# First weights between the pieces of the memory, squares and conv sums on GpSimd, five u blocks loaded ahead of their stage

## The chip, the cores and the metric

The kernel runs on one core of a Trainium2 chip, in one launch. A core has five engines that each work through a list of instructions in order: TensorE (PE, matmuls, with its weight loads as PEld), VectorE (DVE), ScalarE (ACT), GpSimd (POOL) and SyncE (SP), and 16 DMA engines that the transfers of all queues share. The metric is the device time of one execution in microseconds.

## The reference

256 tokens of 1024 numbers pass two blocks. All arithmetic is float32.

```
h = rms_norm(x, norm_g);  mem_h = rms_norm(mem, mem_norm_g)      # 256 x 1024 each
c_glu, c_gate, d_q, d_k, d_v, d_gate, x_q, x_gate, merge = split(h @ w_in)
y_conv = silu(layer_norm(conv31(a * sigmoid(b)) + dw_b)) * silu(c_gate) @ w_conv_proj
y_diff = differential attention(d_q, d_k, d_v), normed, * silu(d_gate) @ w_diff_proj
y_mem  = attention(x_q; k, v = split(mem_h @ w_mem_kv)) * silu(x_gate) @ w_x_proj
x = x + (g0 * y_conv + g1 * y_diff + g2 * y_mem) @ w_out         # g = sigmoid(merge)

h = rms_norm(x, norm_mix);  q, k, v, x_rg, g_rg = split(h @ w_in_2)
x = x + concat(norm(stick breaking attention), norm(rg_lru(conv4(x_rg)) * gelu(g_rg))) @ w_out_2
h = rms_norm(x, norm_ffn)
s = (h @ w_query) . sub_keys                                     # 8 heads, 2 x 128 keys
idx, gate = the 16 best of (top 16 of half 1) + (top 16 of half 2), softmax
x = x + sum_k gate_k * gelu(h . u[idx_k]) * v[idx_k]             # 16384 experts
```

rms_norm divides by the root of the mean square over the 1024 channels; layer_norm needs the mean and the mean square over the channels of the conv's output.

## The kernel before, in words

Channels lie on the 128 partitions, in eight chunks; a tile of one chunk is 128 x 256 (channels x tokens). Every dense product is cut into weight blocks of 1024 x 256, stored as 128 x 2048 and loaded in two halves of 512 KB. There are 94 such blocks of ordinary weights (in_wcat, 188 halves) and then 64 blocks of u and 64 of v, all experts of the last layer.

An ordinary block goes through `prep`: SyncE loads a half (raw), ScalarE rounds it to the short format (whi, L247), VectorE subtracts (wlo = raw - whi, L248), and TensorE multiplies three times: whi with the high part of the activations (hh), wlo with hh, whi with the low part (hl). One block is 48 matmuls into a PSUM tile called lin, of which there are three. `linT` gives channels x tokens, `linN` (L330) tokens x channels. `ahead` starts the preparation of the block behind the one just multiplied.

The start. SyncE loads the memory m_t in four pieces (256 KB each) with the vectors VT behind the first, then the first weights, then x in two halves, tables, and more weights. ScalarE scales m_t by its gain into mgh and rounds it, VectorE forms the rest mgl; ScalarE squares the four pieces, and eight matmuls with a matrix of ones (L439) add up the squares over the channels (tile stat). Then come blocks 0 to 3 (mem_h times the value half of w_mem_kv). Meanwhile x gets its norm, and hh and hl are made from it; blocks 4 and 5 are the first to use them.

The conv. Each of the 31 taps of the first layer's conv is one VectorE instruction per chunk (L533, L535, 248 in all) that accumulates into cacc. The taps lie in a list bg from which some are issued behind each block, so they fill VectorE's time between the wlo subtractions. When all are done, ScalarE squares cacc and TensorE adds cacc and its squares up over the channels (L691 to L699: eight matmuls on cacc, eight on the squares, float32), then VectorE forms mean and variance, ScalarE the reciprocal root (rv, rs, rt). Between them stand the blocks mc1 to mc3 (gates, the sigmoids smc), and behind these four blocks cg0 to cg3.

Each activation function of ScalarE belongs to a table, and a change of table is an instruction of its own (ACT_TABLE_LOAD). A list scheduler sets the order of all instructions on each engine by priorities and estimated ready times, so an edit at one place can change orders at others.

The expert layer. Of the 256 tokens 160 are worked densely: TensorE multiplies them with all 64 blocks of u (L288) and, weighted by the gates, all 64 of v (L1177), in float32, without rounding; these halves are loaded into a ring of 13 tiles, the former raw, whi and wlo tiles (`prep_plain`, L225). The gates come from products A and B (group gp), and VectorE multiplies them in (`mul`, L1155). The other 96 tokens are gathered: GpSimd issues 96 indirect loads of u rows and 96 of v rows (L1186, 512 KB each), VectorE forms a dot product of each u tile (L1193) and accumulates each v tile (L1211). VectorE's list mixes these with the ga operations of L1155, and a gather's buffer comes free only when VectorE has used it. The tile ga is the place for the results of the u blocks.

GpSimd does nothing before 597 us; then it loads fold, copies xG, adds the candidate sums cs of the top-k (L998), and issues the gathers.

## Time and profile before

| | |
|---|---|
| runs | 1292.05, 1288.19, 1291.8 us, median 1291.8 |
| profiled execution | 1291.35 us, span 1289.6 us |
| TensorE busy | 1253.5 us (97% of the span) |
| VectorE busy | 937.0 us (73%) |
| ScalarE busy | 457.3 us (35%) |
| GpSimd busy | 214.6 us (17%) |
| DMA | 340.76 MB, mean 264 GB/s |

A row of the timeline gives the start of an instruction in us from the start of the span, its length, engine, line and operation, output <- inputs by name, the shapes, and in brackets how long the engine was idle before it and what ended that. Where several alike follow each other they stand in one row with their count. Matmul records overlap, so the length of one says less than the distance between them. A digit in the slices is the busy share in tenths of 1289.6 / 40 = 32.2 us. A DMA share of 1 means that all 16 DMA engines are busy.

### The profile page before, as it was taken

What the parts mean: (1) busy time and instruction counts of PE and PEld (TensorE: products, weight loads), DVE (VectorE), ACT (ScalarE), POOL (GpSimd) and SP (SyncE); (2) the same over time, 40 slices, a digit from 0 to 9 for tenths busy, and PEclk for the clock granted to TensorE, in tenths of its full rate; (3) what the DMA queues carried; (4) which work ended last, traced back from release to release, by engine and by line L of the source; (5) the groups of instructions that cost most, each with busy time, mean ns of one, the idle gap of its engine ahead of it and who ended that gap; (6) DMA issues with size and microseconds to landing.
All of it is one profiled execution on the core that took longest, in us unless ns stands there. A gap on an engine that the chain in (4) does not pass through costs nothing.

```text
span 1289.6 us, 24478 instructions
## 1 busy us (share of the span) xinstructions
PE 1253.5 (97%) x9948; PEld 1211.0 (94%) x9948; DVE 937.0 (73%) x1806; ACT 457.3 (35%) x741; POOL 214.6 (17%) x222
## 2 busy tenths in 40 slices
PE   8999999999999999998999899999999999999995
PEld 7999999989999999977999899999999999999884
DVE  6889988888998777855899864588545886445444
ACT  7545677578646556955431100010000000000001
POOL 0000000000000000000013443222342225333331
PEclk9999999999999999999999999999999999999998
DMA  8655443434565664423577999999999999999996
GB/s 294 189 194 182 164 138 124 132 116 147 164 200 161 196 202 157 148 67 99 181 235 240 354 409 409 409 408 363 382 383 342 356 360 392 409 409 408 409 409 231
DMA packets 94865, 340.76 MB, mean 264 GB/s; under 512 B 10576, under 2 KB 12048, under 8 KB 94624
## 3 DMA queue, kind: packets, MB, share of 16 engines
q1 hardware_dynamic: 66752, 237.98, 52.0%
q0 software_dynamic: 28000, 101.22, 20.4%
q8 instruction: 78, 1.28, 0.4%
q14 instruction: 35, 0.29, 0.1%
HBM read 338.01 MB, written 1.05 MB: 263 GB/s over the span
## 4 chain that ended last, share of the span: by engine, by line
PE 43%; issue 20%; DMA 16%; DVE 11%; POOL 6%; ACT 3%; POOLq 0%; SPq 0%; DVEq 0%; ACTq 0%
DMA gat<-in_vrow,gi 10%; PE lin L308 10%; PE lin L307 10%; PE lin L309 10%; POOL gat L1186 6%; DMA gat<-in_urow,gi 5%; DVE acc L1211 2%; PE lin L341 1%; DVE gat L1193 1%; PE lin L343 1%; PE lin L342 1%; DVE wlo L248 1%; PE stat L459 1%; ACT whi L247 1%; DVE I L983 1%
## 5 line engine op out<-in xcount | busy, mean ns | idle before, releaser
L1177 PE MATMUL y<-ga,w 128*128 128x160 f32 x2048 | 293.0, 302 | 5.6 <-DMA w<-in_v 2.8
L1177 PEld LDWEIGHTS y<-ga,w 128*128 128x128 f32 x2048 | 279.9, 190 | 13.3 <-DMA w<-in_v 10.4
L288 PE MATMUL lin<-h3f,w 128*128 128x160 f32 x2048 | 290.5, 302 | 1.7 <-ACT ga L1166 1.7
L288 PEld LDWEIGHTS lin<-h3f,w 128*128 128x128 f32 x2048 | 281.5, 191 | 2.3 <-ACT ga L1166 1.9
L248 DVE TENSOR_TENSOR wlo<-raw,whi 128x1024 fp32r<-128x1024 f32 x188 | 229.1, 1221 | 64.2 <-ACT whi L247 63.5
L247 ACT CAST whi<-raw 128x1024 fp32r<-128x1024 f32 x188 | 196.2, 1049 | 167.2 <-PE lin L308 123.8
L308 PE MATMUL lin<-hl,whi 128*128 128x256 f32 x704 | 200.2, 284 | 0.0
L309 PE MATMUL lin<-hh,wlo 128*128 128x256 f32 x704 | 199.8, 284 | 0.0
L307 PE MATMUL lin<-hh,whi 128*128 128x256 f32 x704 | 199.8, 284 | 0.0
L1211 DVE SCALAR_TENSOR_TENSOR acc<-gat,cG,acc 128x1024 f32<-128x1024 f32 x94 | 120.7, 1284 | 95.3 <-DMA gat<-in_vrow,gi 49.2
L1193 DVE CUSTOM_DVE_ANT_0 gat<-gat,hrow 128x1024 f32<-128x1024 f32 x96 | 116.6, 1224 | 29.8 <-DMA gat<-in_urow,gi 16.2
L1186 POOL DMA_INDIRECT gat<-in_urow,gi x96 | 103.4, 1077 | 198.9 <-DVE sG L1193 188.9
L309 PEld LDWEIGHTS lin<-hh,wlo 128*128 128x128 f32 x704 | 132.6, 188 | 2.2 <-issue 1.9
L308 PEld LDWEIGHTS lin<-hl,whi 128*128 128x128 f32 x704 | 132.6, 188 | 1.7 <-issue 1.4
L307 PEld LDWEIGHTS lin<-hh,whi 128*128 128x128 f32 x704 | 132.5, 188 | 1.4 <-issue 1.0
L1186 POOL DMA_INDIRECT gat<-in_vrow,gi x96 | 93.3, 972 | 162.6 <-DVE acc L1211 127.4
L1166 ACT ACTIVATE ga<-lin 128x320 f32<-128x320 f32 x64 | 27.9, 437 | 249.8 <-PE lin L288 216.7
L535 DVE SCALAR_TENSOR_TENSOR cacc<-ub,VT,cacc 128x256 f32<-128x256 f32 x240 | 103.7, 478 | 0.0
L955 POOL DMA_DIRECT2D fold<-in_con x1 | 0.7, 703 | 596.9 <-DVE gate L924 596.9
L1292 ACT COPY ga<-y 128x160 f32<-128x160 f32 x4 | 1.2, 292 | 236.2 <-PE y L1177 236.2
L1155 DVE SCALAR_TENSOR_TENSOR ga<-gp,ga 128x256 f32<-128x256 f32 (+1 forms) x60 | 29.1, 510 | 74.6 <-PE gp L1144 55.3
L308 PE MATMUL lin<-h3lo,whi 128*128 128x256 f32 x128 | 37.3, 291 | 2.3 <-DVE h3lo L384 2.3
(373 smaller groups left out, 2099.9 us busy)
## 6 DMA issues: line engine op xcount, KB each, us to landing
raw<-in_wcat SPq DMA_DIRECT2D x188, 512.0 KB
w<-in_u SPq DMA_DIRECT2D x128, 512.0 KB
w<-in_v SPq DMA_DIRECT2D x128, 512.0 KB
gat<-in_urow,gi POOLq DMA_INDIRECT x96
gat<-in_vrow,gi POOLq DMA_INDIRECT x96
m_t<-in_memT SPq DMA_DIRECT2D x4, 256.0 KB
xr<-in_xT SPq DMA_DIRECT2D x2, 512.0 KB
kT<-in_keysT SPq DMA_DIRECT2D x1, 1024.0 KB
```

What stands on the lines that cost most here:

```text
L247: nc.scalar.copy(h, raw)
L248: state["sub"] = nc.vector.tensor_sub(l, raw, h.bitcast(F32))
L288: nc.tensor.matmul(ps[:, a], ws[a][:, c * P:(c + 1) * P], x[:, c], start=c == 0, stop=c == 7)
L307: nc.tensor.matmul(ps[:, a], wh, ah[:, c], start=(a, c) in first, stop=False)
L308: nc.tensor.matmul(ps[:, a], wh, al[:, c], start=False, stop=False)
L309: nc.tensor.matmul(ps[:, a], wl, ah[:, c], start=False, stop=(a, c) in last)
L535: nc.vector.scalar_tensor_tensor(cacc[:, c], s, w, cacc[:, c], op0=ALU.mult, op1=ALU.add)
L1155: state["dve"] = nc.vector.scalar_tensor_tensor(g_[:, :, tl], p_, 1.0 / GSCALE, g_[:, :, tl], op0=ALU.mult, op1=ALU.mult)
L1177: nc.tensor.matmul(yT[c // 2][:, c % 2, :D], ws[a][:, c * P:(c + 1) * P], g[:, a], start=False, stop=i == 63 and (a, c % 2) == (1, 1))
L1186: nc.gpsimd.indirect_dma_start(g, None, src, bass.IndirectOffsetOnAxis(gi[:, 0, k:k + 1].bitcast(U32), 0))
L1193: nc.vector.tensor_tensor_reduce(out=g, in0=g, in1=h, scale=1.0, scalar=0.0, op0=ALU.mult, op1=ALU.add, accum_out=sG[:, k:k + 1])
L1211: state["sum"] = nc.vector.scalar_tensor_tensor(acc[m], g, cG[:, k:k + 1], acc[m], op0=ALU.mult, op1=ALU.add)
```

## The change

The edits are these.

- The first weights' halves are loaded between the pieces of m_t, the second block's weights ahead of x. Block 0 is multiplied channel by channel for both token halves.
- The four squares of m_t and two of the adds go to GpSimd; TensorE adds up the first piece's squares ahead of block 0 and the sum of the other three behind it. The norm of m_t is formed there.
- The sums over cacc are formed while the taps run: ScalarE squares a pair of chunks as soon as it is done, GpSimd (for the first three pairs) or VectorE (the last) adds up rx and sqs. Three matmuls remain of sixteen.
- ScalarE's operations for la (a constant of the second block) stand behind the last merge sigmoid.
- u blocks 11 to 15 (LATE) are not loaded through the ring, but by ten transfers that GpSimd issues ahead of the fold load, into parts of ga that are not yet in use.

```diff
         NW = len(STREAM)
+        LATE = range(NW + 11, NW + 16)
         RING = ("raw",) * 5 + ("whi",) * 4 + ("wlo",) * 4
 
         def prep_plain(i):
             ws = []
             for a in range(2):
-                tag = RING[(2 * (i - NW) + a) % len(RING)]
+                tag = RING[(2 * (i - NW - (len(LATE) if i >= LATE.stop else 0)) + a) % len(RING)]
                 w = spool.tile([P, 1024], F32, name="w", tag=tag, bufs=RING.count(tag))
                 nc.sync.dma_start(w, srcs[i][:, a * 1024:(a + 1) * 1024])
                 ws.append(w)
             prepared[i] = ws
 
-        def prep(i):
+        def load(i, a):
+            raw = spool.tile([P, 1024], F32, name="raw", bufs=5)
+            nc.sync.dma_start(raw, srcs[i][:, a * 1024:(a + 1) * 1024])
+            return raw
...
-            for j in range(i, min(i + (5 if i >= NW else 1), len(srcs))):
+            n = 5 + (i - 1 in LATE) if i >= NW else 1
+            for j in [j for j in range(i, len(srcs)) if j not in LATE][:n]:
...
+                nc.tensor.matmul(ps[:, t], xh, wh, start=(t, c) in first, stop=False)
+                nc.tensor.matmul(ps[:, t], xl, wh, start=False, stop=False)
+                nc.tensor.matmul(ps[:, t], xh, wl, start=False, stop=(t, c) in last)
...
+            def m_load(k):
+                nc.sync.dma_start(m_t[:, 2 * k:2 * k + 2], memT[:, 2 * k:2 * k + 2])
+
+            m_load(0)
             nc.sync.dma_start(VT, vec)
-            for k in range(1, 4):
-                nc.sync.dma_start(m_t[:, 2 * k:2 * k + 2], memT[:, 2 * k:2 * k + 2])
-            prep(0)
+            raws = [load(0, 0)]
+            m_load(1)
+            m_load(2)
+            raws.append(load(0, 1))
+            m_load(3)
+            raws1 = [load(1, a) for a in range(2)]
             for k in range(2):
                 nc.sync.dma_start(x_t[:, 4 * k:4 * k + 4], xT[:, 4 * k:4 * k + 4])
+            mgh, mgl = bigt("mgh", F32R), bigt("mgl", F32R)
+
+            def m_gains(a):
+                for c in range(4 * a, 4 * a + 2):
+                    gain_col(m_t, "mem_norm_g", mgh, mgl, c)
+
+            m_gains(0)
+            prep(0, raws, lambda a: [gain_col(m_t, "mem_norm_g", mgh, mgl, c) for c in (2, 3, 4, 5)] if a else None)
+            for c in (6, 7):
+                gain_col(m_t, "mem_norm_g", mgh, mgl, c)
+
+            stm = statp()
+            msq = [smt("sqs", 512, 1), smt("sq"), smt("sq")]
+            for k in range(4):
+                q = msq[min(k, 2)] if k < 3 else smt("gate", 512, 3)
+                nc.gpsimd.tensor_mul(q.rearrange("p (a b) -> p a b", a=2), m_t[:, 2 * k:2 * k + 2],
+                                     m_t[:, 2 * k:2 * k + 2])
+                if k > 1:
+                    nc.gpsimd.tensor_add(msq[1], msq[1], q)
+                if k == 0:
+                    for b in range(2):
+                        nc.tensor.matmul(stm[:, :T], ONES, q[:, b * T:(b + 1) * T], start=b == 0, stop=False)
+            rm = smt("rm", T, 1)
+            prep(1, raws1)
...
-            for c in range(0, NC, 2):
-                rms_sq(m_t, stm, c, NC)
-            rstd_of(stm[:, :T], 1.0 / 1024, T, out=rm)
-            rmt = tok_scalar(rm, "rmt")
             vm = big.tile([P, 2, 1024], F32, name="vm", tag="big")
             hh, hl = bigt("hh", F32R), bigt("hl", F32R)
             for j in range(4):
-                ps = linN((mgh, mgl))
+                ps = linN((mgh, mgl), j == 0)
+                if j == 0:
+                    for b in range(2):
+                        nc.tensor.matmul(stm[:, :T], ONES, msq[1][:, b * T:(b + 1) * T], start=False, stop=b == 1)
+                    rstd_of(stm[:, :T], 1.0 / 1024, T, out=rm)
+                    rmt = tok_scalar(rm, "rmt")
...
+            def conv_sums(j):
+
+                def f():
+                    e = nc.gpsimd if j < 3 else nc.vector
+                    x = cacc[:, 2 * j:2 * j + 2]
+                    sq = smt("sq" if j else "sqs", 512, 2 if j else 1)
+                    nc.scalar.square(sq.rearrange("p (a b) -> p a b", a=2), x)
+                    if j == 0:
+                        sums.append(sq)
+                        e.tensor_add(rx, x[:, 0], x[:, 1])
+                    else:
+                        for k in range(2):
+                            e.tensor_add(rx, rx, x[:, k])
+                        e.tensor_add(sums[0], sums[0], sq)
+                return f
+
             for j in range(4):
                 pb = linT(h)
                 sg = smt("sig")
@@ -546,6 +604,7 @@
                 for jj in range(KT):
                     for c in (2 * j, 2 * j + 1):
                         bg.append((0.394, tap(c, jj)))
+                bg.append((0.0, conv_sums(j)))
...
-            for c in range(0, NC, 2):
-                sq = smt("sq")
-                nc.scalar.square(sq.rearrange("p (a b) -> p a b", a=2), cacc[:, c:c + 2])
-                for k in range(2):
-                    nc.tensor.matmul(s1[:, :T], ONES, cacc[:, c + k], start=c + k == 0, stop=c + k == 7)
-                    nc.tensor.matmul(s2[:, :T], ONES, sq[:, k * T:(k + 1) * T], start=c + k == 0, stop=c + k == 7)
+            nc.tensor.matmul(s1[:, :T], ONES, rx, start=True, stop=True)
+            for k in range(2):
+                nc.tensor.matmul(s2[:, :T], ONES, sums[0][:, k * T:(k + 1) * T], start=k == 0, stop=k == 1)
...
+        late = [g[:, o:o + 32].rearrange("p a b -> p (a b)") for g, o in ((ga[0], 32), (ga[1], 0))]
+        late = [x[:, k * 1024:(k + 1) * 1024] for x in late for k in range(len(LATE))]
+        for k, i in enumerate(LATE):
+            for a in range(2):
+                nc.gpsimd.dma_start(late[2 * k + a], srcs[i][:, a * 1024:(a + 1) * 1024])
+            prepared[i] = late[2 * k:2 * k + 2]
```

The order of GpSimd's instructions before, up to its first add (m_t is the memory, cs the top-k's candidate sums):

```order
L1305 MEMSET const-uint8-127 128x1
L1313 UNCONDITIONAL_BRANCH
L955 DMA fold<-in_con 128x96
L956 COPY xG<-xr 128x768
L998 ISA
L998 TENSOR_TENSOR cs<-V_7191 128x256 x11
```

And now:

```order
L522 ISA
L522 TENSOR_TENSOR sqs<-m_t 128x512
L522 TENSOR_TENSOR sq<-m_t 128x512 x2
L525 TENSOR_TENSOR sq<-sq 128x512
L522 TENSOR_TENSOR gate<-m_t 128x512
L525 TENSOR_TENSOR sq<-sq,gate 128x512
L589 TENSOR_TENSOR rx<-cacc 128x256
L592 TENSOR_TENSOR rx<-rx,cacc 128x256 x2
L593 TENSOR_TENSOR sqs<-sqs,sq 128x512
L592 TENSOR_TENSOR rx<-rx,cacc 128x256 x2
L593 TENSOR_TENSOR sqs<-sqs,sq 128x512
L1005 DMA ga_7127<-in_u 128x1024 x5
```

GpSimd now has six instructions on m_t at the start, seven on the conv's sums, and ten loads of u, all ahead of fold.

ScalarE in the stretch of the differential attention between the norm of one head pair (rv, rs, rt) and the copy of its neighbour's probabilities (sig<-att), before:

```order
L374 ACTIVATE rv<-stat,VT 128x512
L662 ACTIVATE gate<-lin 128x512
L375 ACT_TABLE_LOAD
L375 ACTIVATE rs<-rv 128x512
L376 ACT_TABLE_LOAD
L376 ACTIVATE rs<-rs 128x512
L570 ACTIVATE pp,z<-s,nm 128x128 x2
L377 ACTIVATE rt<-rs 128x512
L643 COPY sig<-att 128x384
L570 ACTIVATE pp,z<-s,nm 128x256 x2
L247 CAST whi<-raw 128x1024 x4
```

And now:

```order
L387 ACTIVATE rv<-stat,VT 128x512
L388 ACT_TABLE_LOAD
L388 ACTIVATE rs<-rv 128x512
L254 CAST whi<-raw 128x1024
L721 ACT_TABLE_LOAD
L721 ACTIVATE gate<-lin 128x512
L629 ACT_TABLE_LOAD
L629 ACTIVATE pp,z<-s,nm 128x128 x2
L389 ACTIVATE rs<-rs 128x512
L702 COPY sig<-att 128x384
L629 ACTIVATE pp,z<-s,nm 128x256 x2
L254 CAST whi<-raw 128x1024
```

The function of gate now stands between rs and rs, with a table of its own; a cast (whi) has moved ahead of the copy, rt behind it.

ScalarE around the norm of the conv (cacc is the conv's result, smc the sigmoids of blocks mc1 to mc3), before:

```order
L696 ACTIVATE sq<-cacc 128x512
L247 CAST whi<-raw 128x1024
L374 ACTIVATE rv<-nrm,VT 128x256
L375 ACTIVATE rs<-rv 128x256
L247 CAST whi<-raw 128x1024
L376 ACTIVATE rs<-rs 128x256
L377 ACTIVATE rt<-rs 128x256
L714 ACT_TABLE_LOAD
L714 ACTIVATE smc<-lin 128x512 x2
L247 CAST whi<-raw 128x1024 x2
L714 ACTIVATE smc<-lin 128x512
```

And now:

```order
L586 ACTIVATE sq<-cacc 128x512
L254 CAST whi<-raw 128x1024 x2
L387 ACTIVATE rv<-nrm,VT 128x256
L388 ACTIVATE rs<-rv 128x256
L254 CAST whi<-raw 128x1024
L389 ACTIVATE rs<-rs 128x256
L390 ACTIVATE rt<-rs 128x256
L770 ACT_TABLE_LOAD
L770 ACTIVATE smc<-lin 128x512 x3
L773 ACT_TABLE_LOAD
```

The three sigmoids stand together behind the table load; before, two casts stood between the second and the third.

## Rows read from the trace of the kernel before

**Rows 1.** Section 2 of the page: TensorE, VectorE and the DMA engines, in 40 slices of 32 us

```profile
PE   8999999999999999998999899999999999999995
...
DVE  6889988888998777855899864588545886445444
...
DMA  8655443434565664423577999999999999999996
```

**Rows 2.** What TensorE waited for from 38 to 345 us: total us, times, longest

```profile
PE lin L341 <- ACT y L655: 0.6, 1, 0.6
```

**Rows 3.** Timeline of the start: start us, us, engine line op, [idle before, releaser]

```profile
8.36 0.91 ACT L412 ACTIVATE mgh<-m_t,VT 128x256 fp32r<-128x256 f32 x2 [0.49 <-DMA m_t<-in_memT]
...
8.90 0.88 DVE L413 SCALAR_TENSOR_TENSOR mgl<-m_t,VT,mgh 128x256 fp32r<-128x256 f32 x2 [0.52 <-ACT mgh L412]
...
9.79 1.03 ACT L247 CAST whi<-raw 128x1024 fp32r<-128x1024 f32 x1
...
13.04 0.47 PE L342 MATMUL lin<-wlo,mgh 128*128 128x256 f32 x1
...
18.95 0.60 PE L420 MATMUL stat<-ONES,rm 1*128 1x1 f32 x4
```

**Rows 4.** Timeline, VectorE and GpSimd, between 626 and 720 us

```profile
626.70 1.22 DVE L248 TENSOR_TENSOR wlo<-raw,whi 128x1024 fp32r<-128x1024 f32 x1
...
626.87 1.53 POOL L998 TENSOR_TENSOR cs<-V 128x256 f32<-128x256 f32 x1 [25.58 <-DVE V L988]
...
708.93 1.23 DVE L1193 CUSTOM_DVE_ANT_0 gat<-gat,hrow 128x1024 f32<-128x1024 f32 x1 [1.67 <-DMA gat<-in_urow,gi]
...
719.09 0.62 POOL L998 TENSOR_TENSOR cs<-V 128x256 f32<-128x256 f32 x1 [1.56 <-DVE V L988]
...
719.25 1.53 DVE L1193 CUSTOM_DVE_ANT_0 gat<-gat,hrow 128x1024 f32<-128x1024 f32 x1
```

**Rows 5.** Timeline, ScalarE and TensorE, between 311 and 319 us

```profile
311.77 1.28 ACT L375 ACT_TABLE_LOAD   x1
...
316.31 0.61 ACT L377 ACTIVATE rt<-rs 128x512 f32<-128x512 f32 x1
...
316.84 0.45 ACT L643 COPY sig<-att 128x384 f32<-128x384 f32 x1
...
317.34 0.70 PE L644 MATMUL att<-sig,vd 128*128 128x256 f32 x2
```

**Rows 6.** One of the groups of TensorE from 340 to 404 us: xcount of records

```profile
L698 PE MATMUL stat<-cacc,ONES 128*128 128x256 f32 x16 | 4.6, 378 | 0.0
```

**Rows 7.** Timeline, TensorE and ScalarE, between 399 and 412 us

```profile
399.11 0.59 PE L698 MATMUL stat<-cacc,ONES 128*128 128x256 f32 x2
...
401.99 1.02 PE L699 MATMUL att<-sq,ONES 128*128 128x256 f32 x4
...
405.28 1.05 ACT L247 CAST whi<-raw 128x1024 fp32r<-128x1024 f32 x1 [0.33 <-PE lin L308]
...
406.23 0.41 ACT L376 ACTIVATE rs<-rs 128x256 f32<-128x256 f32 x1
...
407.11 1.28 ACT L714 ACT_TABLE_LOAD   x1
...
411.88 0.58 ACT L714 ACTIVATE smc<-lin 128x512 f32<-128x512 f32 x1
```

**Rows 8.** Stretches: length, busy us (records) of each engine, clock, DMA share, GB/s

```profile
590.00:595.00 5.00, 5.00 (x44) 4.97 (x43) 2.74 (x5) 3.66 (x6) 0.00 (x0) 1.00 0.00 0
...
1175.00:1200.00 25.00, 25.00 (x187) 25.00 (x186) 12.35 (x10) 0.00 (x0) 9.47 (x10) 1.00 1.03 408
```

**Rows 9.** Instructions of L1155: duration ns, first and last start us

```profile
L1155 DVE SCALAR_TENSOR_TENSOR ga<-gp,ga x60: 412/425/693, 816.3 to 1068.4; 128x256 f32<-128x256 f32 x40, 128x512 f32<-128x512 f32 x20
```

**Rows 10.** Instructions of L1177, and what ended the idle time before them: us, times

```profile
L1177 PE MATMUL y<-ga,w x2048: 299/299/403, 968.7 to 1274.1; 128*128 128x160 f32 x187
...
  DMA w<-in_v: 13.2, 25
```

38 lines of the change are left out of this document (19 added, 19 removed).

## The prediction

> **What bounds the kernel now.** I read the slices first, then the waits of TensorE, then the timelines at the three places that the change touches. The slices show TensorE at nine tenths or more in nearly every slice [rows 1]; it is the engine that sets the end, and between 38 and 345 us it waits for 0.6 us in all [rows 2]. So a new wait in that stretch cannot hide behind an old one: it adds to the end in full. The exceptions are the start, before the matmuls run without a break, and the end: the DMA digit is 9 from 709 us on with hardly a break, and between 968 and 1274 us the matmuls of the v blocks (L1177) lose 13.2 us in 25 waits for weights [rows 1, 10]. At 1175 us the DMA engines are full (share 1.03, 408 GB/s) [rows 8]. The last stretch is therefore set by bytes, everything before it by TensorE and by what can hold it up.
>
> The profiled execution took 1291.35 us, 1.75 around a span of 1289.6; the median of the runs shown is 1291.8. I sum against 1291.35 and compare with the median. About 0.3% (3.9 us) is what a measurement of this kernel can tell from no change.
>
> **The start.** In bytes, the second piece of m_t now stands where its fourth stood in SyncE's order (1.23 MB issued up to and with it), and that one landed about 8.3 us [rows 3]; the first half of the first weights now lands before that, instead of at 9.8 [rows 3]; the fourth piece now stands where their second half stood, 0.52 MB or 1.3 us behind 9.8, some 11.1 us. ScalarE loses four squares and casts each half as it comes. Block 0 could then run from about 8.3 to 15.2 instead of 13.04 to 18.95 [rows 3]. Behind it the rows of x land 1.05 MB, about 2.5 us at the GB/s of the saturated stretch [rows 8], later than before, and their norm (the hh and hl of block 4) then becomes what block 4 and 5 wait for. Free of other trouble I get 2.0 us less at the end of block 5.
>
> But the squares and adds of m_t go to GpSimd, and TensorE waits for them twice: its first two matmuls, and two more directly behind block 0, with all later blocks queued behind. Six GpSimd operations on 512 elements a row: I take 1.24 us each, twice the 0.62 of the 256 wide add (L998) [rows 4]; bounds 0.9 and 3.0, the latter twice the slow add. The slow add is the point. At 626.87 an add took 1.53 us: VectorE had begun a wlo subtraction (two operands in SBUF) at 626.70, which ended at 627.92, and 0.6 us after that the add was over. At 719.09 the add came first, and the dot product that VectorE began at 719.25 took 1.53 instead of 1.23 [rows 4]. So such operations of the two engines take turns here. From 8.3 us on the turns are: five GpSimd operations (6.2), six mgl operations of VectorE (0.44 each, from 0.88 for two [rows 3]: 2.6) and two wlo (2.4), together 11.2 us, and everything is ready at about 19.5. The last twelve matmuls of block 0 (0.12 each, 48 from 13.04 to 18.95 [rows 3]) and two stat matmuls (0.86) then end near 21.4, where before block 1 began at about 19.5; the norm of x, whose matmul stands in the middle of block 2, adds another 1 us of waiting in block 5. That is +3.0 instead of -2.0. I take +3.0, range -2.0 to +5.0 (VectorE keeps its turn through all of its run, GpSimd ends last).
>
> The Trainium skill's page "SBUF — State Buffer", section "Who interferes with whom", says that a VectorE instruction with two SBUF inputs and a GpSimd instruction that reads SBUF share a port pair, which whoever comes first holds for its whole instruction. The two rows agree with it, but show it for wlo and the dot product only, not for mgl; by the rule it holds there as well and the sum is the one above; without it the sum is 5 us lower. This rule speaks against moving squares to GpSimd while VectorE prepares weights.
>
> **The middle (300 to 360 us).** The scheduler has put ScalarE's work in another order (second order excerpt). Before, the copy "sig<-att" at 316.84 ended at 317.29, and the matmul that reads it began at 317.34 [rows 5]: no slack. In the new order the copy has one table load (1.28) and one cast (1.05) more ahead of it and one rt (0.61) less [rows 5, 7]: 1.7 us later, of which I charge 1.3. The next copy has rt and five casts ahead of it, and behind it stand a table load and the sigmoids that free a PSUM tile of lin: another 1 to 4 us if TensorE gets there first. I take +3.0 for the stretch, range 0 to 6 (0 if ScalarE arrives early enough by itself).
>
> **The sums of the conv.** Before: 8 matmuls on cacc (16 records [rows 6]) and 8 on its squares, two groups alike; two records more cost 0.43 us (1.02 for four against 0.59 for two) [rows 7], so a matmul of two records costs 0.43. Three remain: 13 x 0.43 = 5.6 us of TensorE saved. The adds on GpSimd (five of 256, two of 512, 5.6 us in all) delay VectorE's taps by turns; its digits there are 8 and 9 of 10 [rows 1], and TensorE waits for none of them, so I charge 0. What is lost: the three stat matmuls used to stand 68 lin matmuls before the first matmul of the block cg0, now 22. That matmul waits for smc to free a PSUM tile, and ScalarE's chain before smc (third excerpt) is now late: cast 1.05, rs 0.41, rt about the same, table load 1.28, smc 0.58 [rows 7] = 3.8 us from the end of the block ahead of cg0, all of it stall. Net -1.8; range -5.6 (the chain is done in time, as before) to +1 (VectorE's last adds of rx are late too).
>
> **The late blocks.** Ten transfers of 0.52 MB (u blocks 11 to 15) leave SyncE's queue and go on GpSimd's, from about 590 us, where the DMA engines are at 0.00 [rows 8]. They take about 13 us at 408 GB/s there; TensorE needs the first of them only behind eleven other u blocks, so they are early. Behind them on GpSimd are the fold load, the xG copy and the first cs add at 626.87: covered. What does it save? While TensorE works on these five blocks no ring tile comes free, so SyncE's queue stands and later weights come no earlier. What can run ahead is the gathers, and those are held by VectorE's own order: 60 ga operations (L1155) from 816.3 to 1068.4 [rows 9] each wait for TensorE. Up to the last of them, VectorE's order had 96 dots and 8 accumulations; now 96 and 12. So four gathers, 4 x 0.52 = 2.1 MB, are out of the way at 1068, and the stretch behind, which is full to the end, is shorter by 2.1 MB / 0.408 = 5.1 us. Range 0 (see the rival) to 5.24 MB / 0.408 = 12.8 (all of the bytes moved).
>
> The la chain of ScalarE (three short operations, with table loads) now stands behind the last merge sigmoid; the casts behind it are a block ahead of TensorE, which hides it: 0, or two table loads (2.6) if that cover is gone.
>
> **Sum.** +3.0 + 3.0 - 1.8 - 5.1 = -0.9: 1290.4 us.
>
> **Rivals.**
> Squares hidden: GpSimd and VectorE do not hold each other up at mgl, and the middle stays covered: -2.0 + 0 - 1.8 - 5.1 = -8.9, 1282.5 us. For it: only two slow operations in the trace. Against it: both slow ones met a partner with two operands.
> Relief not passed on (slower): the four gathers only empty the DMA engines earlier, because the last weights and the gathers that VectorE accumulates at its own pace set the end, not bytes. Then the tail gives 0: +3.0 + 3.0 - 1.8 = +4.2, 1295.6 us. It decides if the waits for w in the v blocks stay at 13 us. For it: the transfers taken out of 705 to 735 us were not waited for. Against it: the share of 1.03.
> Full relief: all 12.8 us come back at the end: 1291.35 + 4.2 - 12.8 = 1282.8 us. For it: the same bytes in a full stretch. Against it: the ring.
>
> **How the numbers follow.** Chances: forecast 0.38, squares hidden 0.30, relief not passed on 0.24, full relief 0.08. The forecast by itself spans 1287 to 1294. Of it about 0.07 is faster by over 0.3% (below 1287.9) and 0.02 slower (above 1295.7); of the hidden squares 0.28 faster; of no relief 0.12 slower and 0.12 the same; of full relief 0.07 faster. That gives 0.42 faster, 0.43 within 0.3%, 0.15 slower. The range 1281 to 1297 leaves out the lower edge of the first and third rival and the upper edge of the second.
>
> **What would show it.** Start: the first lin matmul near 8 us, a wait of TensorE for GpSimd's sq behind block 0, GpSimd's operations on m_t at 1.2 to 2.5 us each and wlo over 1.3 us; without them the rival has it. Middle: waits of TensorE on ScalarE's sig between 310 and 360 us, some 3 us. Conv: a wait of about 3.8 us for smc at the first matmul of cg0. Tail: DMA busy at 590 to 605 us, twelve accumulations before the last ga operation, and waits for w in L1177 near 8 us. I am wrong if TensorE's waits before 662 us do not add up to this, or if the v stretch is as long as before.

## The result and the profile after

The changed kernel takes 1301.38 us (median of 6 runs, 1297.48 to 1304.79); the kernel before takes 1291.92 beside it (6 runs). The ratio is 1.0081, with a 95% interval of 1.0066 to 1.0095: slower by 10.5 us by the ratio and by 9.5 between the medians, where 0.9 us less had been forecast, and beyond the upper end of the range. The profiled execution took 1301.54 us, its span is 1299.8.

When the same instruction starts, after less before, shows where the time went:

| place | before, us | later by, us |
|---|---|---|
| first sigmoid of the conv gates (L541) | 47.5 | 2.0 |
| blocks around 78 us | 78 | 0.5 |
| first gate of the differential attention (L662) | 293.9 | 0.7 |
| first merge sigmoid (sig, L674) | 328.9 | 5.3 |
| smc ahead of the conv's norm (L691) | 392.4 | 7.1 |
| first and last smc behind it (L714) | 408.4, 411.9 | 10.3, 7.7 |
| first scores of the stick breaking attention (L840) | 539.5 | 9.7 |
| first xr of the last norm (L925) | 597.2 | 10.9 |
| first gp (L1073) | 620.7 | 14.4 |
| first matmul of the v blocks (L1177) | 968.7 | 12.7 |
| last matmul of the v blocks | 1274.1 | 10.0 |

So the loss comes in steps: 4.6 from 294 to 329 us, 1.8 up to the conv's norm, 2.6 from there to the scores, 4.7 from there to gp. From gp to the end 4.4 come back. The slices answer to [rows 1]; PEclk is the granted clock in tenths:

```profile
PE   7999999999898999999899899999999999999995
...
PEclk9999999999899999999899999999999999999998
DMA  8565543444455465423766789999999999999995
```

There is little to see in them: the eleventh and the thirteenth slice of TensorE (from 325 and 390 us) read 8 instead of 9, and the granted clock has an 8 in the eleventh. DMA reads 7, 6, 6, 7 and 8 from 617 to 780 us, where it read 5, 7, 7 and then nines: the late blocks' bytes are out of that stretch and have moved ahead of it. Ten microseconds in 1300 hide in such digits. The waits of TensorE from 300 to 430 us show more (us in all, times, longest); [rows 2] had nothing of this kind up to 345 us:

```profile
PE lin L315 <- ACT smc L770: 3.7, 1, 3.7
PE att L703 <- ACT sig L702: 2.5, 2, 1.4
PE lin L315 <- ACT sig L733: 1.5, 1, 1.5
```

The timeline of the middle, answering to [rows 5]:

```profile
318.03 0.46 ACT L702 COPY sig<-att 128x384 f32<-128x384 f32 x1
...
318.54 0.70 PE L703 MATMUL att<-sig,vd 128*128 128x256 f32 x2 [1.40 <-ACT sig L702]
...
334.80 0.58 PE L315 MATMUL lin<-hh,whi 128*128 128x256 f32 x1 [1.51 <-ACT sig L733]
335.18 0.42 PE L316 MATMUL lin<-hl,whi 128*128 128x256 f32 x1
335.39 0.41 PE L317 MATMUL lin<-hh,wlo 128*128 128x256 f32 x1
```

The copy that began at 316.84 before begins at 318.03, and the matmul that had no slack waits 1.40 us. A second pair of the same kind waits 1.07. Then the first merge sigmoid frees its PSUM tile late, and TensorE waits 1.51. The rows behind it start 0.21 us apart, where 0.12 is the usual distance of such matmuls. The stretches (length, busy us and records of the five engines, granted clock, DMA share, GB/s) say why:

```profile
330.00:340.00 10.00, 7.43 (x40) 6.99 (x39) 9.51 (x19) 4.80 (x7) 0.74 (x1) 0.71 0.53 178
...
420.00:430.00 10.00, 10.00 (x77) 10.00 (x76) 6.99 (x14) 7.95 (x14) 0.00 (x0) 0.86 0.25 85
```

From 330 to 340 us TensorE works 7.4 of 10 us and its granted clock is 0.71, so part of the stretch is at the lower of its two levels; in the 6 us behind the wait some 22 matmuls stand 0.21 apart, about 2 us lost. The wait for smc ends at 419.3, and behind it the clock falls too: 0.86 from 420 to 430 us, where the kernel before has 1.00, and about 1.4 us lost. That wait is the forecast one: 3.7 us, where 3.8 had been worked out.

The start, answering to [rows 3, 4]:

```profile
6.86 3.02 POOL L522 TENSOR_TENSOR sq<-m_t 128x512 f32<-128x512 f32 x2 [1.74 <-DMA m_t<-in_memT]
...
7.20 0.58 PE L354 MATMUL lin<-whi,mgh 128*128 128x256 f32 x1
...
8.90 3.48 DVE L426 SCALAR_TENSOR_TENSOR mgl<-m_t,VT,mgh 128x256 fp32r<-128x256 f32 x4
12.30 2.06 DVE L255 TENSOR_TENSOR wlo<-raw,whi 128x1024 fp32r<-128x1024 f32 x1
...
12.62 0.41 PE L354 MATMUL lin<-whi,mgh 128*128 128x256 f32 x1
12.83 0.41 PE L355 MATMUL lin<-whi,mgl 128*128 128x256 f32 x1
...
13.38 0.28 PE L355 MATMUL lin<-whi,mgl 128*128 128x256 f32 x1
13.50 0.28 PE L356 MATMUL lin<-wlo,mgh 128*128 128x256 f32 x1
...
27.36 1.03 PE L410 MATMUL stat<-sqs,ONES 128*128 128x256 f32 x4
```

Block 0 begins at 7.20 us (forecast: near 8; before, its first matmul was at 11.35 and the unbroken run began at 13.04). GpSimd's two squares take 1.04 and 1.87 beside VectorE; four mgl operations take 3.48 together, where 1.76 would follow from [rows 3] (the single records: 1.25 and 1.50 beside a square and an add of GpSimd, then twice 0.47; of all eight three are long, up to 1.51); and the second wlo takes 2.06 instead of 1.22 [rows 4]. The first matmuls stand 0.21 us apart, the later ones 0.12; the granted clock reads 9 tenths or more in this slice all the same. The wait for GpSimd's second sum, forecast directly behind block 0, does not occur: its stat matmuls run at 17.26. Block 1 begins at 17.93, where it began at 19.48 before. But the sums for the norm of x run at 27.36, where they ran at 21.02 before; TensorE then waits 0.5 us for hl at 40.3, and the matmuls around it are slow, some 1.3 us in all. So the lead is gone at 78 us (0.5 late).

The late blocks, answering to [rows 4, 8]; the first row holds eight of the ten loads:

```profile
607.99 4.42 POOL L1005 DMA_DIRECT2D ga<-in_u  x8 [259.97 <-PE lin L335]
...
618.65 0.83 POOL L1021 COPY xG<-xr 128x768 f32<-128x768 f32 x1
...
617.68 4.07 DVE L420 SCALAR_TENSOR_TENSOR h3f<-xr,VT,rx 128x256 f32<-128x256 f32 x8
```

```profile
620.00:625.00 5.00, 2.86 (x13) 2.86 (x14) 5.00 (x14) 5.00 (x10) 0.00 (x0) 0.58 1.02 408
```

The loads were forecast from about 590 us. They were issued at 607.99, because their place in ga is free only when TensorE has read what lay there before (lin, L335). The last two, at 615.27 and 616.56, wait until earlier ones have landed, and behind them stand the fold load and the xG copy. So the copy falls on VectorE's last norm: h3f takes 4.07 us for eight instead of 3.26, all of the difference in one operation of 1.30 us (the median is 0.47). TensorE works 2.86 of the 5 us behind 620, and the granted clock there is 0.58. The kernel before has such a pause as well (1.46 of 5 us from 605 on, 0.66 from 610 to 615), so only the difference counts. The gathers' accumulations and the v blocks, answering to [rows 9, 10]:

```profile
L1220 DVE SCALAR_TENSOR_TENSOR ga<-gp,ga x60: 414/425/693, 829.3 to 1081.0; 128x256 f32<-128x256 f32 x40, 128x512 f32<-128x512 f32 x20
```

```profile
L1242 PE MATMUL y<-ga,w x2048: 299/299/403, 981.4 to 1284.1; 128*128 128x160 f32 x187
...
  DMA w<-in_v: 11.5, 25
```

The last ga operation starts at 1081.0 (12.6 later), and up to it VectorE has made 12 accumulations instead of 8: four more, as forecast. But from there to the last matmul of the v blocks it is 203.1 us instead of 205.7, 2.6 less, where 5.1 had been forecast. The v blocks take 302.7 us instead of 305.4, and 11.5 us of waiting for w are left of 13.2, where 8 had been forecast.

### The profile page after: what moved, and what is told of

It reads as the page before. It is cut to its first block, busy times and chain, and to the rows that moved or that the text cites. A ratio compares the mean times of both kernels' runs of the same rounds, so it can differ in the third digit from the quotient of the medians.

```text
span 1299.8 us, 24440 instructions
## 1 busy us (share of the span) xinstructions
PE 1252.0 (96%) x9914; PEld 1210.5 (93%) x9914; DVE 944.9 (73%) x1809; ACT 461.1 (35%) x741; POOL 231.5 (18%) x245
## 3 DMA queue, kind: packets, MB, share of 16 engines
q0 software_dynamic: 29440, 106.46, 21.4%
## 4 chain that ended last, share of the span: by engine, by line
PE 41%; issue 19%; DMA 18%; DVE 11%; POOL 5%; ACT 5%; POOLq 0%; SPq 0%; DVEq 0%; ACTq 0%
DMA gat<-in_vrow,gi 13%; PE lin L316 10%; PE lin L315 10%; PE lin L317 10%; DMA gat<-in_urow,gi 5%; POOL gat L1251 5%; DVE wlo L255 1%; ACT whi L254 1%; DVE gat L1258 1%; PE lin L356 1%; PE lin L354 1%; PE lin L355 1%; DVE acc L1276 1%; PE stat L472 1%; PE sc L897 1%
## 5 line engine op out<-in xcount | busy, mean ns | idle before, releaser
L296 PE MATMUL lin<-h3f,w 128*128 128x160 f32 x1888 | 265.1, 300 | 0.0
L296 PEld LDWEIGHTS lin<-h3f,w 128*128 128x128 f32 x1888 | 257.7, 190 | 0.3 <-DMA w<-in_v 0.2
L1251 POOL DMA_INDIRECT gat<-in_urow,gi x96 | 99.6, 1038 | 192.9 <-DVE sG L1258 168.0
L1005 POOL DMA_DIRECT2D ga<-in_u x10 | 5.5, 569 | 263.6 <-PE lin L335 260.0
L592 POOL TENSOR_TENSOR rx<-rx,cacc 128x256 f32<-128x256 f32 x4 | 4.9, 1220 | 223.7 <-DVE cacc L575 223.6
## 6 DMA issues: line engine op xcount, KB each, us to landing
w<-in_u SPq DMA_DIRECT2D x118, 512.0 KB, 11.7
```

What stands on the lines that cost most here:

```text
L296: nc.tensor.matmul(ps[:, a], ws[a][:, c * P:(c + 1) * P], x[:, c], start=c == 0, stop=c == 7)
L1251: nc.gpsimd.indirect_dma_start(g, None, src, bass.IndirectOffsetOnAxis(gi[:, 0, k:k + 1].bitcast(U32), 0))
```

## The experiments

Each kernel was timed against the kernel before on the same chip. Ratios have their 95% intervals in brackets; "in us" is the ratio less 1 times the median before. Two kernels were timed on two chips, and against the kernel before they read 3.0 and 5.4 us (c_alone), 2.4 and 5.0 (c_filled). So a difference of 2 us between kernels that ran on different chips shows nothing.

**The three parts alone.** Each of these is the kernel before with one part of the change.

```
f_alone, against the changed kernel (the sums of the conv as before too):
-        LATE = range(NW + 11, NW + 16)
+        LATE = range(0)
...
-                bg.append((0.0, conv_sums(j)))
c_alone, against the kernel before (with conv_sums, and the three matmuls):
+                bg.append((0.0, conv_sums(j)))
l_alone, against the kernel before (with the loop over late):
+        LATE = range(NW + 11, NW + 16)
```

> Only the start's part of the change: the order of the first loads, block 0 channel by channel, the squares of m_t on GpSimd. Theory (the start's edit reorders ScalarE far behind it): the start itself costs 0.5 us, the stretch from 300 to 395 us costs some 6 us through new waits of TensorE for the copies sig and the clock that falls behind them, so 6 to 7 us slower than before, about 1298.5. Rival (the late order comes from the conv's squares, which ScalarE now does earlier): the start alone costs 0.5 us, 1292.5.

> Only the conv sums formed while the taps run. Theory: nothing between 300 and 390 us, then a wait of 3.7 us for smc plus slower clock behind it against 5.6 us of matmuls saved: 1 to 3 us slower, about 1294. Rival (the conv's squares upset ScalarE's order): some 9 us slower, 1301.

> Only the five late blocks on GpSimd's queue. Theory: 1 us lost at 608 to 635 us, where the xG copy now meets VectorE's h3f, 4 us won in the u and v stretches by four gathers fewer at the end: 3 us faster, about 1289. Rival (the ten transfers hold up the queries' weights and cost 3.5 us there): 0 to 1 us faster, 1291.5.

f_alone: 1302.86 against 1291.05 us, 1.0091 [1.0072, 1.0109]: 11.7 us slower. c_alone: 1293.65, 1.0023 [1.0012, 1.0033]: 3.0 slower. l_alone: 1290.3, 0.9994 [0.9982, 1.0006]: no difference that can be told. So the start's part alone costs as much as the whole change (the intervals overlap), and 4 us of it are waits that lie 300 us behind it: f_alone waits the same 2.5 us for the copies and 1.5 for the merge sigmoid. The waits of c_alone from 300 to 430 us, and matmuls behind its wait for smc:

```profile
PE lin L315 <- ACT smc L738: 4.2, 1, 4.2
PE lin L317 <- DVE wlo L255: 2.2, 2, 1.7
```

```profile
413.85 0.42 PE L317 MATMUL lin<-hh,wlo 128*128 128x256 f32 x1
414.06 0.41 PE L315 MATMUL lin<-hh,whi 128*128 128x256 f32 x1
```

The wait is 4.2 us, and 25 matmuls behind it start 0.21 apart, until 418.7.

**Is it the start, or the order behind it?** start_old_order has f_alone's start, but from the first conv gate on ScalarE, VectorE and TensorE are held to the order of the kernel before. order_alone is the reverse: the start of before, and f_alone's order behind it.

```diff
+        made = {int(i.name[2:]): i for i in nc.all_instructions() if i.name[:2] == "I-"}
+        for row in ROWS:
+            row = [made[a + k * d] for a, d, n in row for k in range(n) if a + k * d in made]
+            for a, b in zip(row, row[1:]):
+                tc.add_manual_dep(b, a.name, mybir.DependencyInfo(
+                    mybir.DependencyClass.NoSync, mybir.DependencyReason.DATA), reason="order")
...
```

ROWS are the instructions of each engine in the order wanted.

> The start's edit alone, as in f_alone, but from the first conv gate on ScalarE, VectorE and TensorE are held to the order in which their instructions stood in the kernel before. Theory (what f_alone lost between 300 and 430 us and behind it, about 8 of its 11.8 us, comes from the order in which the scheduler then puts ScalarE's and TensorE's work, not from the start itself): only the start's own loss is left, 2.9 us in f_alone's trace at 200 to 300 us, so 1294 us (1291.5 to 1295.5), and TensorE waits less than 0.5 us between 300 and 430 us, with a granted clock of 1.00 there. Rival (something that the start leaves behind, such as later weight loads or a lower clock, slows the middle whatever the order): 1299 us or more, with waits of 3 us or more in that stretch.

> The kernel before, its start untouched; from the first conv gate on ScalarE, VectorE and TensorE are held to the order in which their instructions stand in f_alone (the mirror of start_old_order). Theory (the order by itself makes most of f_alone's loss): TensorE waits near 315 to 340 us for sig as in f_alone, 2.5 and 1.5 us, and the time is 1298 us (1296 to 1300), some 7 to 9 over before. Rival (the order costs only together with the start's delay): 1293 us or less.

start_old_order: 1294.08 against 1290.45, 1.0026 [1.0011, 1.0040], 3.4 us. The view of TensorE's waits is empty from 300 to 430 us. order_alone: 1299.58 against 1290.17, 1.0062 [1.0042, 1.0082], 8.0 us, with the waits of the changed kernel at the same two places, although nothing at all is changed in what is computed or loaded:

```profile
PE att L644 <- ACT sig L643: 2.5, 2, 1.4
PE lin L307 <- ACT sig L674: 1.5, 1, 1.5
```

Its instructions are 5.5 us later at 340 us, 4.5 at 392 (smc), 6.3 at sc (the first scores) and 8.7 at gp. Together 3.4 + 8.0 = 11.4 of the 11.7 of f_alone. The 4.0 us of waits are half of the order's cost; 1.5 more come directly behind them, where the granted clock is 0.83 from 330 to 340 us. The remaining 3.2 arise between 340 us and gp, 2.4 of them behind the first scores. Of these, 1.6 lie in the sums of squares for the last norm: from their first to their last matmul 5.1 us pass instead of 3.5, with a wait of 2.0 instead of 1.5 and a lower clock behind it. The rest was not taken apart.

**What the start itself costs.** start_no_gpsimd is start_old_order with the squares on ScalarE and the adds on VectorE.

```diff
-                nc.gpsimd.tensor_mul(q.rearrange("p (a b) -> p a b", a=2), m_t[:, 2 * k:2 * k + 2],
-                                     m_t[:, 2 * k:2 * k + 2])
+                nc.scalar.square(q.rearrange("p (a b) -> p a b", a=2), m_t[:, 2 * k:2 * k + 2])
...
-                    nc.gpsimd.tensor_add(msq[1], msq[1], q)
+                    nc.vector.tensor_add(msq[1], msq[1], q)
```

> As start_old_order, but ScalarE squares the four pieces of m_t and VectorE adds two of them up; GpSimd does nothing at the start. In start_old_order the four mgl operations beside GpSimd take 1.07 us each and the two wlo 1.84 and 2.29, where alone they take 0.44 and 1.2. Theory (the two engines take turns at such operations): mgl at 0.43 to 0.45 and wlo at 1.2 us from the first on; the second wlo is ready near 13 us instead of 15.4, block 0 ends 1 to 2 us earlier, and the time is 1 to 2 us below start_old_order: 1292.5 us. Rival (they are slow because of the loads that fill memory at the same time, DMA share 1.0): mgl and wlo stay above 0.8 and 1.6 us, and the time equals start_old_order, 1294, or more.

1291.88 against 1290.72, 1.0009 [0.9998, 1.0020]. That is 2.2 us less than with GpSimd, but on another chip and with intervals that overlap, so a gain is not shown. What VectorE's timeline shows is that the operations are shorter, first with GpSimd's squares (start_old_order), then without:

```profile
8.96 4.26 DVE L426 SCALAR_TENSOR_TENSOR mgl<-m_t,VT,mgh 128x256 fp32r<-128x256 f32 x4
13.14 2.29 DVE L255 TENSOR_TENSOR wlo<-raw,whi 128x1024 fp32r<-128x1024 f32 x1
```

```profile
9.05 1.67 DVE L426 SCALAR_TENSOR_TENSOR mgl<-m_t,VT,mgh 128x256 fp32r<-128x256 f32 x4
...
11.49 1.23 DVE L255 TENSOR_TENSOR wlo<-raw,whi 128x1024 fp32r<-128x1024 f32 x1 [0.17 <-ACT whi L254]
...
30.33 1.03 PE L410 MATMUL stat<-sqs,ONES 128*128 128x256 f32 x4
```

Four mgl go from 4.26 us back to 1.67, wlo from 2.29 to 1.23: the turns of the two engines. What that is worth at the end stays open. Block 1 begins at 17.91 here and at 18.90 in start_old_order, but also at 17.93 in the changed kernel, with GpSimd's squares. The third row is the sum for the norm of x, at 30.33, later still than in the changed kernel (27.36), and that costs: TensorE waits 0.71 and 0.50 us for hl, and 3.5 us are lost around it against 1.3 in start_old_order. At the first merge sigmoid this trace is 3.1 us late, that of start_old_order 1.6; the spans are 1292.0 and 1292.2. Single traces do not resolve more: best (below) keeps the start of before, but waits for the third piece of m_t until 8.55 us (ScalarE took it up at 6.98 before) and is 2.9 us late at 47.5.

start_warm asked about the slow pace of the first matmuls. It is start_old_order with nine matmuls on constants ahead of all others:

```diff
+            warm = attp()
+            for k in range(9):
+                nc.tensor.matmul(warm[:, :P], ONES, ONES, start=True, stop=True)
```

> As start_old_order, and ahead of everything TensorE multiplies the matrix of ones by itself nine times (nothing reads the result). In the changed kernel and in f_alone the first 28 matmuls of block 0 stand 0.213 us apart and the later ones 0.12, and the change comes 8 to 11 us after TensorE's first instruction; in the kernel before the square sums run at the slow pace while TensorE waits for data anyway (eight in 4 us, later four in 1.1). Theory (the pace is TensorE's own, after it was idle, and starting block 0 five us earlier therefore gains only half): with TensorE busy from about 1 us block 0 runs at 0.12 from 9 us on, and the first matmul that reads hh comes about 2 us earlier than in start_old_order: 1292 us (2 less than it). Rival (the slow pace is set by what the matmuls read, freshly loaded tiles or the three other engines on the same memory): the pace stays at 0.21 up to 13 us or more, and the time equals start_old_order.

1293.01 against 1290.45, 1.0021 [1.0009, 1.0033]: 0.6 us less than without, inside the uncertainty. TensorE's timeline:

```profile
1.07 4.21 PE L493 MATMUL att<-ONES 128*128 128x128 f32 x18 [1.07 <-DVE ONES L490]
...
9.60 0.28 PE L354 MATMUL lin<-whi,mgh 128*128 128x256 f32 x1
9.72 0.28 PE L355 MATMUL lin<-whi,mgl 128*128 128x256 f32 x1
...
15.72 0.38 PE L356 MATMUL lin<-wlo,mgh 128*128 128x256 f32 x1 [2.16 <-DVE wlo L255]
...
17.31 0.41 PE L356 MATMUL lin<-wlo,mgh 128*128 128x256 f32 x1
17.52 0.41 PE L354 MATMUL lin<-whi,mgh 128*128 128x256 f32 x1
```

The idea on the pace holds: after the added matmuls those of block 0 stand 0.12 apart at 9.6 us. It gained nothing, because TensorE then waits for VectorE's wlo: 2.16 us at 15.72 (3.5 in all), and behind the wait it is at 0.21 again. Without the added matmuls the same row started at 15.49. So in this trace VectorE's wlo sets the end of block 0, not the pace.

**The conv's sums.** c_dropped asked whether the saved matmuls are worth anything. It is the kernel before without the squares and the twelve matmuls of the first six chunks, and with nothing in their place (so the sums lack these chunks).

```diff
-            for c in range(0, NC, 2):
+            for c in range(6, NC, 2):
...
-                    nc.tensor.matmul(s1[:, :T], ONES, cacc[:, c + k], start=c + k == 0, stop=c + k == 7)
+                    nc.tensor.matmul(s1[:, :T], ONES, cacc[:, c + k], start=c + k == 6, stop=c + k == 7)
...
```

> The kernel before without the sums of conv chunks 0 to 5: three of four squares and twelve of the sixteen matmuls (on cacc and on the squares) are left out, nothing takes their place, GpSimd has no part in it. They took 12 x 0.43 = 5.2 us of TensorE. Theory (ten of them stood between 344 and 349 us, where VectorE is late with the low halves wlo, and filled time in which TensorE would have waited; and the norm's chain then comes later against block cg0): the saved time comes back as waits for wlo from 345 to 362 us and one for smc near 405: 1291 us (1289.5 to 1294). Rival (what is taken off TensorE counts in full): 1286 us, and no waits for wlo over 0.5 us.

1291.41 against 1290.45, 1.0008 [0.9996, 1.0020]. As forecast there is no gain, but of the two causes given only the second shows, the wait for smc; the waits from 335 to 430 us are these:

```profile
PE lin L307 <- ACT smc L714: 3.7, 1, 3.7
PE lin L309 <- DVE wlo L248: 0.7, 1, 0.7
```

Only 0.7 us are lost on wlo. Its blocks are 3.0 us early at 392 us; then it waits 3.7 for smc, and at sc it is 2.1 late. VectorE's timelines name what sets that chain, first in the kernel before, then in c_dropped: the last conv tap (cacc) and the mean (rm), from which the norm is worked out.

```profile
397.32 0.48 DVE L535 SCALAR_TENSOR_TENSOR cacc<-ub,VT,cacc 128x256 f32<-128x256 f32 x1
...
401.60 0.42 DVE L701 TENSOR_SCALAR rm<-stat 128x256 f32<-128x256 f32 x1 [1.38 <-PE stat L698]
```

```profile
399.24 0.48 DVE L535 SCALAR_TENSOR_TENSOR cacc<-ub,VT,cacc 128x256 f32<-128x256 f32 x1
...
403.56 0.42 DVE L701 TENSOR_SCALAR rm<-stat 128x256 f32<-128x256 f32 x1 [1.41 <-PE stat L698]
```

In c_alone the last tap is at 401.4 and rm at 407.1, in the changed kernel at 406.8 and 411.8. TensorE gets to the norm earlier, VectorE's 248 taps do not: in c_dropped one more wlo stands ahead of the last. In c_alone the new adds come on top: three taps that meet GpSimd's take 0.96 us instead of 0.48, all taps together 1.5 us more, and VectorE's own adds stand between the last tap and rm.

c_mc1 takes the wait away by another order: the sigmoid of mc1 stands ahead of the change of ScalarE's table, so that its PSUM tile is free in time.

```diff
-            table(nc.scalar.activation(smc[:, 0:2], linT(h), AF.Sigmoid), LN_EXP)
+            for j in range(2):
+                last = nc.scalar.activation(smc[:, 2 * j:2 * j + 2], linT(h), AF.Sigmoid)
+            table(last, LN_EXP)
...
-            for j in range(1, 4):
+            for j in range(2, 4):
```

> The conv's sums alone, as in c_alone, but the sigmoid of block mc1 is taken together with that of the first gate block, ahead of the table change for the norm; before, it stood behind the norm's reciprocal root. Theory (ScalarE's chain behind the late sums holds a PSUM tile of lin, TensorE waits 4.2 us for it, and behind the wait it works at a lower granted clock, 0.66 from 410 to 420 us, which costs about 2.5 more): without the wait both go: 1287 us (1285.5 to 1289), clock 1.00 at 405 to 430. If only the wait goes and the clock stays low: 1289.5. Rival (the next step of that chain, cn or the gates cg, is late by as much): 1292 to 1294.

1289.46 against 1290.45, 0.9994 [0.9982, 1.0005]: the wait is gone, and the clock reads 1.00 from 400 to 420 us. In medians it is 4.2 us less than c_alone, as much as the wait, and 5.9 less than c_again, the same kernel on the same chip as c_mc1 (below). c_filled leaves the wait and keeps TensorE busy in it with 18 matmuls on constants, against the lower clock behind:

```diff
+            with tc.issue_after(state["last"].ins):
+                fill = attp()
+                for k in range(18):
+                    i = nc.tensor.matmul(fill[:, :P], ONES, ONES, start=True, stop=True)
```

> The conv's sums alone, as in c_alone, and between the last matmul of block mc3 and the first of block cg0, where TensorE waits 4.2 us for smc, it multiplies the matrix of ones by itself 18 times (about 0.21 us each, 3.8 us; nothing reads the result). The wait stays as long as it was, only it is filled. In c_alone the 25 matmuls behind the wait stand 0.213 us apart instead of 0.118, 2.4 us lost, at a granted clock of 0.64 to 0.67. Theory (the clock falls because TensorE stood idle): the clock stays at 1.00 from 410 to 420 us, the matmuls behind it stand 0.12 apart, and the time is 2.4 us less than c_alone's 1293.65: 1291 us (1290 to 1292). Rival (the clock falls for another reason, such as what TensorE did before, or power): 1293.5 us and 0.65 again.

1293.44 against 1290.72, 1.0019 [1.0009, 1.0028]. In its trace the fill works:

```profile
407.93 4.18 PE L744 MATMUL att<-ONES 128*128 128x128 f32 x36
412.29 0.38 PE L315 MATMUL lin<-hh,whi 128*128 128x256 f32 x1 [0.18 <-ACT smc L740]
412.51 0.28 PE L318 MATMUL lin<-hl,whi 128*128 128x256 f32 x1
412.63 0.28 PE L319 MATMUL lin<-hh,wlo 128*128 128x256 f32 x1
```

The matmuls behind stand 0.12 apart, and sc is 1.6 late instead of 4.6 in c_alone. The medians of the two kernels differ by 0.2 us only. Both were run once more side by side:

> The same kernel as c_alone, beside c_filled_again on one chip. Expected as before, 1293.6 us.

> The same kernel as c_filled, beside c_again on one chip. If the fall of the clock behind the wait, which c_alone's trace shows and c_filled's does not, is in most executions: 1.5 to 2.5 us less than c_again. If it is in few of them, or given back later: the same time within 1 us.

1295.39 and 1294.6 us against 1290.17, 1.0042 [1.0029, 1.0056] and 1.0039 [1.0025, 1.0052]: 0.8 apart. The trace of c_again has 14 slow matmuls behind the wait, that of c_alone 25. The fill is thus worth 0.2 and 0.8 us in the two pairs, with intervals that allow anything from nothing to some 2 us. How often the clock falls in executions without a profile stays open.

**The late blocks.** l_copy_first is l_alone with the fold load and the xG copy ahead of the last two of the ten loads.

```diff
+            with ExitStack() as s:
+                if k == 4:
+                    s.enter_context(tc.issue_after(nc.gpsimd.tensor_copy(xG, xr[:, :, D:]).ins))
+                    nc.gpsimd.dma_start(fold, con0[:, 2 * P:])
+                for a in range(2):
+                    nc.gpsimd.dma_start(late[2 * k + a], srcs[i][:, a * 1024:(a + 1) * 1024])
```

> As the late blocks alone, with GpSimd's xG copy ahead of the last two of the ten loads, where VectorE waits for the norm. Theory: VectorE's eight h3f operations take 3.3 us again instead of 4.1, so 0.8 us faster than the late blocks alone, about 1288. Rival (it is the transfers that slow h3f): h3f stays at 4.1 us and the time is that of the late blocks alone.

1288.46 against 1291.05, 0.9972 [0.9960, 0.9984]: 3.6 us faster than before, and 1.8 better than l_alone (medians, on one chip). VectorE's h3f in l_alone, then in l_copy_first:

```profile
604.26 4.01 DVE L415 SCALAR_TENSOR_TENSOR h3f<-xr,VT,rx 128x256 f32<-128x256 f32 x8
```

```profile
605.00 3.26 DVE L415 SCALAR_TENSOR_TENSOR h3f<-xr,VT,rx 128x256 f32<-128x256 f32 x8
```

Eight operations took 4.01 us while GpSimd copied xG beside them, and 3.26 when the copy had been made earlier. That is 0.75 of the 1.8; the fold load moved as well, and the rest is not assigned.

**All mended, and the best of the parts.** all_mended is the whole change with the three mends: the order of before from the first conv gate to the merge gates, c_mc1's sigmoid and l_copy_first's copy. best leaves out the start's part and every held order, and keeps the conv's sums with c_mc1's sigmoid, the moved la, and the late blocks with the copy first.

> The whole change with the three causes mended that the runs point to: from the first conv gate to the end of the merge gates ScalarE, VectorE and TensorE keep the order of the kernel before (the conv's sums, free of it, apart); the sigmoid of mc1 stands ahead of the norm's table change, as in c_mc1; and the copy of xG and the fold load stand ahead of the last two of the ten late loads, as in l_copy_first. Theory (these three make up the loss, the start about +2 to +3 remains): against the changed kernel's 1301.4 us the middle gives 5 to 6 back (waits on sig and the low clock behind them), smc 5 to 6, the copy 1.8, together about 12: 1289.5 us (1287 to 1292). Rival (the parts disturb each other in a way that none of the three covers): 1294 us or more.

> The parts of the change that were not seen to lose, with their causes mended, and the start as in the kernel before: the conv's sums with the sigmoid of mc1 ahead (c_mc1), ScalarE's operations for la behind the last merge sigmoid, the five late blocks with the xG copy ahead of the last two loads (l_copy_first). If gains add up: -1.0 (c_mc1) and -2.6 (l_copy_first), 1287 us against 1290.5, a ratio of 0.997. If the late blocks' gain is the same relief at the end that an earlier arrival of the v blocks already takes (the tail is set by bytes): 1288.5, as l_copy_first alone.

all_mended: 1292.86 against 1290.72, 1.0013 [0.9999, 1.0026], 3.4 us more than expected and above the expected range. 8.5 of the 12 us hoped for came back; its start is 2.7 us late in its trace, and it still waits 1.7 for wlo and 1.7 for odh between 345 and 400 us. best: 1285.57, 0.9955 [0.9939, 0.9971]: 5.8 us faster than the kernel before and 15.8 faster than the changed one.

## Why the prediction was wrong, point by point

- **The middle, +3.0: this step failed.** It charged the copies and the merge sigmoid, and the trace has just these waits, 4.0 us of them (1.4 and 1.1 for the copies, 1.5 for the PSUM tile). But it read one place of a new order and stopped. The order by itself costs 8.0 us (order_alone): 5.5 by 340 us, in those waits and in the slow matmuls behind them, which had no term, and 3.2 more up to gp. For the stretch alone the range of 0 to 6 held (4.6 us by 329 us, 4.9 by the last merge sigmoid at 381); for what lay behind it there was nothing. The order shown ahead of the prediction covers two stretches of ScalarE; the rest of the list had changed as well.
- **The start, +3.0: met in size by luck, not by its working.** start_old_order costs 3.4 us (1.4 to 5.2). The turns are there. The Trainium skill's page "SBUF — State Buffer", section "Who interferes with whom", had been held to apply to mgl too: it does, with four operations in 1.67 us alone and in 3.48 to 4.26 beside GpSimd. But the working let the turns delay block 0, to 21.4 us with its stat matmuls (its terms add up to 21.8; and the slow add of [rows 4] ended 0.48 us behind wlo, not 0.6). In the changed kernel block 1 begins at 17.93, 1.5 earlier than before, and the forecast wait behind block 0 did not occur. What shows is the smaller term, the late norm of x (charged 1 us; a wait for hl of 0.5, some 1.3 lost around it), and in the changed kernel's trace only 0.7 us are lost by 294 us. Whether the turns cost anything at the end is open, and the slow pace of the first matmuls was not in the working.
- **The conv's sums, -1.8: wrong in sign (+3.0; +5.4 in c_again).** The wait for smc was sized well (3.7 in the whole, 4.2 alone, against 3.8). What failed is the 5.6 us of matmuls: c_dropped takes twelve of them away and gains nothing, since the norm's chain starts with VectorE's last tap. Work that TensorE no longer does ahead of it becomes waiting at smc. On top came the adds that delay the taps, a term put at 0 (1.5 us of taps, and rm 5.5 us late in c_alone against 2.0 in c_dropped), and the clock behind the wait, which had no term (about 2.2 us lost in c_alone, 1.2 in c_again).
- **The late blocks, -5.1: the four gathers came, the relief behind them did not.** Behind the last ga operation the stretch is 203.1 us long instead of 205.7. In the five traces with late blocks it is 203.1 to 204.5, in seven others of kernels without them 203.9 to 207.6 (204.4 in order_alone), so 5.1 us by bytes are not shown there. That 4.4 us came back between gp and the end proves little: in c_again, without late blocks, it is 4.2. "Covered" failed as well: the loads began at 608 and not at 590, and the copy came beside VectorE's last norm. Alone the part gives 0.8, inside its interval, with the copy moved 3.6; the trace of l_copy_first gains 3.7 between gp and the first v matmul and 1.1 from there on. So a gain is shown, its place is not the forecast one, and its cause is open. The rival "relief not passed on" is not refuted: the waits for w only fell to 11.5 instead of 8.
- **la, 0:** moved in best along with the rest; not tried alone.
- **The sum.** By ratios the parts give 11.7 + 3.0 - 0.8 = 13.9; the whole costs 10.5. The 3.4 between them are no more than the intervals of the four numbers allow, so whether the parts add up is open.

The slower rival was priced at 1295.6, from the tail. The slower outcome had other causes: the order first, then the conv's sums.

## What to carry to other kernels

When a scheduler places the instructions, price the whole new order behind an edit, engine by engine, at each place where TensorE had no slack, and hold the order of before in one experiment: it tells the edit from its echo. Work saved on the busiest engine is worth nothing ahead of a wait that another engine's chain sets; look up which instruction starts that chain first. A cheap instruction on an idle engine has a price if a busy one reads the same memory at that moment, and the same instruction a few microseconds earlier may be free.

## What the runs showed of the hardware that was not expected

- A GpSimd copy with a single input (xG) slows VectorE's operations with two inputs as well: one h3f took 1.23 to 1.30 us where the others took 0.48, and the copy takes 0.83. So it waits out the copy, as three mgl of the changed kernel waited for a square or an add of GpSimd (1.25 to 1.51, 0.47 in the median).
- The first matmuls of block 0 in the changed kernel stand 0.21 us apart until 13.26 us although the granted clock reads 1.00 there; with nine matmuls ahead of them (start_warm) the pace is 0.12 by 9.6 us, and behind a wait of 2.16 us it is 0.21 again.
- Behind the waits of 3.7 to 4.2 us for smc the granted clock fell in every trace that has one: 0.50 to 0.54 in the 2 us behind it (changed kernel, c_alone, c_again, c_dropped). Behind the wait of 1.51 us for sig it was 0.50 in the changed kernel and in order_alone, and 1.00 in f_alone, which has the same wait.
